# The state scan of a hybrid layer on one core: tables group by group, products for two groups at a time

## The chip, the cores and the metric

The kernel runs on one core of a Trainium2 chip. The metric is device microseconds of one execution, lower is better. A core has a matrix engine (PE in the profile; PEld is its weight load), a vector engine (DVE), a scalar engine (ACT), a general engine (POOL) and a queue that issues transfers (SP). Each works through its own list of instructions in order. The lists are made when the kernel is built: a scheduler places what the code records, and the code can pin an order.

## The reference

One layer of a streaming model for 256 frames of a new stream and 32 frames of a running one, 288 columns together:

```python
xn   = rmsnorm(x, norm_mix_pre)
proj = xn @ w_in                    # [u_pool 1024 | z 2048 | xBC 2560 | dt 32]
y_pool = pool_mixer(u_pool)         # trailing means, then a small matmul
xBC  = silu(causal_dwconv(xBC))     # xs 2048, B 256, C 256
y    = ssd_scan(xs, dt, A, B, C, h0) + D * xs      # 32 heads of 64
y    = y * silu(z);  y = y * rsqrt(mean(y*y)) * g   # mean per half of the heads
x    = x + rmsnorm([y_pool, y] @ w_out)
up   = rmsnorm(x) @ w_up;  f = (silu(conv(gate)) * conv(value)) @ w_down
x    = x + rmsnorm(f)
```

All is float32. The big products are made from two reduced parts of each operand: `hi` (rounded) and `lo` (the rest), as hi·hi + hi·lo + lo·hi.

## The kernel before

Columns of the activations are the free dimension (288), features are the partitions. A large product is a *projection* of 256 output features: 16 blocks of 128 inputs, three matmuls each, for two accumulators (`acc`, a ring of five PSUM banks). Its weights come in two transfers `raw` of 1 MB on the SP queue (ring of four), and each is split in two pieces: ACT rounds `whi` (L129), DVE subtracts for `wlo` (L130). Both are rings of four, so the split runs at most four pieces ahead of PE. One piece feeds 24 matmuls (L135, L136, L137). When a projection ends, DVE takes its two accumulators out (`ebuf` at L341/L342 for xs, `z` at L517).

The scan is done in eight groups of four heads by `ssd_four(q)`. A group fetches the decay exponents `gb`, the state `h0t` and the time-major inputs `xw` (written shortly before as `blocks`, DVE transposes at L171, through DRAM tensor `xs_d`). ACT makes the table `m`: twelve Relu (L471) and one Exp (L474). DVE scales `xw` (L466), `ce` (L463) and `m` (L476). PE then makes 16 small products into two banks `py` (L483 to L489, of the three-bank ring `aux`), in plain float32, with 64-column weights. The profile has two records for each of these float32 matmuls. DVE adds `py` to `xs` (L492).

The eight groups run between the projections. The code calls projections 1 to 7 (xs) and then 8 to 15 (z); `XS_RATE` and `Z_RATE` say after which of them a group is recorded:

```python
XS_RATE = (0, 0, 0, 1, 0, 1, 0, 1)
Z_RATE = (1, 0, 1, 0, 1, 1, 1, 0)
```

Nothing pins the products; the scheduler puts them where it finds their inputs ready. `gb`, `xw`, `h0t`, `ce` and `m` are rings of two.

Ahead of the scan stand nine transposes `ptok` of 32-row tiles (L420 to L422), which turn exponents `g`, steps `dt` and decays `dec` to time-major `tok` and `tokd`, and six float32 products `pcb` (L437 to L439) for the table `cbt`. After a group, the gate multiplies `xs` by silu(z) (L523, L526) and sums squares into `gsum`; when eight tiles are done, `gate_rstd(0)` makes a product `psum_g` (L496), a root on ACT, a reciprocal on DVE (L237), and eight multiplies (L578).

Of the kernel before, what the change touches and what calls it, by code (L numbers as in the profile page):

```python
# [8 lines left out]
F32 = mybir.dt.float32  # L9
F32R = mybir.dt.float32r  # L10
AF = mybir.ActivationFunctionType
ALU = mybir.AluOpType
# [4 lines left out]
P = 128  # L17
TC = {"schedule_with_timeline_sim": True}
D_MODEL = 2048
NP_ = 256  # L20
NS = 32
NT = NP_ + NS
# [3 lines left out]
HEADS = 32  # L26
# [3 lines left out]
NX = D_SSD // P  # L30
# [5 lines left out]
HALF = NF // 2  # L36
MW = 416
EVAC = 100
XS_RATE = (0, 0, 0, 1, 0, 1, 0, 1)
Z_RATE = (1, 0, 1, 0, 1, 1, 1, 0)  # L40


@with_exitstack
def body(
# [25 lines left out]
    act, dve, pool, pe, sp = nc.scalar, nc.vector, nc.gpsimd, nc.tensor, nc.sync  # L70
# [7 lines left out]
    acc_ps = ctx.enter_context(tc.tile_pool(name="acc_ps", bufs=5, space=PSUM))  # L78
# [3 lines left out]
    def aux(shape, name):  # L82
        return aux_ps.tile(shape, F32, tag="aux", name=name)
# [81 lines left out]
            after = nxt  # L165
        return accs

    def blocks_out(d, t, src, pool_):

        s = pool_.tile([P, NT], F32, tag="blocks", bufs=1, name="blocks")  # L170
        dve.transpose(s, src)  # L171
# [9 lines left out]
    mean = const.tile([P, P], F32, name="mean")  # L181
# [16 lines left out]
    for i in range(NE):  # L198
        e = const.tile([P, 326], F32, name=f"ebuf{i}")
# [12 lines left out]
    rstd = const.tile([P, NT], F32, tag="spread", bufs=3, name="rstd")  # L212
# [4 lines left out]
    start = ExitStack()  # L217
# [35 lines left out]
    for kb, n in chunks:  # L253
# [19 lines left out]
        for k in range(kb, kb + n):  # L273
# [19 lines left out]
            for m in range(6):  # L293
                c = slice(m * P, (m + 1) * P)
# [5 lines left out]
    p_ = aux([P, NT], "pdt")  # L300
# [18 lines left out]
    mp = mixer.enter_context(tc.tile_pool(name="mixer", bufs=1))  # L319
# [9 lines left out]
    cw = pah[:, 0:80].rearrange("p (r t) -> p r t", t=NXC)  # L329
    cb_ = pah[:, 80:100]  # L330
    n_conv = [0]
    more = [mp.tile([P, 326], F32, name=f"ebuf{NE + i}") for i in range(2)]
    for e in more:
        pool.memset(e, 0.0)

    def conv_in(i, p_):

        e = (ebuf + more)[n_conv[0] % (NE + 2)]
        n_conv[0] += 1
        with tc.high_priority(offset=EVAC):  # L340
            dve.tensor_tensor(e[:, 3:259], p_[:, :NP_], rstd[:, :NP_], op=ALU.mult)  # L341
            dve.tensor_tensor(e[:, 262:294], p_[:, NP_:], rstd[:, NP_:], op=ALU.mult)  # L342
        pool.tensor_copy(e[:, 259:262], hist_c[:, :, i])
        return e

# [72 lines left out]
    for b, (go, o) in enumerate(((0, 0), (256, P), (288, NT - P))):  # L418
        p_ = aux([P, 3, HEADS], "ptok")
        pe.transpose(p_[:, 0, :], g[:, go : go + P], id32)  # L420
        pe.transpose(p_[:, 1, :], dt[:, o : o + P], id32)
        pe.transpose(p_[:, 2, :], dec_s if b == 2 else dec[:, o : o + P], id32)  # L422
        dve.tensor_copy(tok[:, b, :, :], p_[:, 0:2, :])
        dve.tensor_copy(tokd[:, b, :], p_[:, 2, :])

    bc = []
    for i in range(4):
# [4 lines left out]
    cbt = mp.tile([P, 2, MW], F32, name="cbt")  # L432
    pool.memset(cbt, 0.0)
    for gi in range(2):
        blocks_out(b_d, gi, bc[gi], mp)
# [10 lines left out]
    xs = []  # L446
    elast = const.tile([P, HEADS + 32], F32, name="elast")

    def ssd_four(q):

        c = slice(2 * P * q, 2 * P * q + 2 * P)
        gb = mp.tile([P, 4, MW], F32, tag="gb", bufs=2, name="gb")
        sp.dma_start(out=gb, in_=g_d[4 * q : 4 * q + 4, :].unsqueeze(0).broadcast_to([P, 4, MW]))
        h0t = mp.tile([P, 2 * P], F32, tag="h0t", bufs=2, name="h0t")
        sp.dma_start(out=h0t, in_=state_ssd[:, c])
        xw = mp.tile([P, 3, 2 * P], F32, tag="xw", bufs=2, name="xw")
        sp.dma_start(out=xw[:, 0:2, :], in_=xs_d[:NP_, c].rearrange("(b p) c -> p b c", p=P))
        sp.dma_start(out=xw[:, 2, :], in_=xs_d[NT - P :, c])
        ce = mp.tile([P, 4, NS], F32, tag="ce", bufs=2, name="ce")
        act.activation(ce, gb[:, :, 384:], AF.Exp)  # L460
        act.activation(elast[:, 4 * q : 4 * q + 4], gb[:, :, MW - 1], AF.Exp)
        cs = bc[2 + q // 4][:, NP_:]
        dve.tensor_tensor(ce, ce, cs.unsqueeze(1).broadcast_to([P, 4, NS]), op=ALU.mult)  # L463
        w = tok[:, :, 1, 4 * q : 4 * q + 4].unsqueeze(3).broadcast_to([P, 3, 4, 64])
        x4 = xw.rearrange("p b (r q) -> p b r q", r=4)
        dve.tensor_tensor(x4, x4, w, op=ALU.mult)  # L466
        m = mp.tile([P, 4, MW], F32, tag="m", bufs=2, name="m")
        for j in range(4):
            h = 4 * q + j
            for b, (lo_, hi_) in enumerate(((0, 256), (256, 384), (384, MW))):  # L470
                act.activation(  # L471
                    m[:, j, lo_:hi_], gb[:, j, lo_:hi_], AF.Relu, bias=tok[:, b, 0, h : h + 1], scale=-1.0
                )
        act.activation(m, m, AF.Exp, scale=-1.0)  # L474
        gi = q // 4
        dve.tensor_tensor(m, m, cbt[:, gi : gi + 1, :].broadcast_to([P, 4, MW]), op=ALU.mult)  # L476
        ys = [aux([P, NT], "py") for _ in range(2)]
        for k in range(4):
            for j in range(4):
                c = slice(64 * j, 64 * j + 64)  # L480
                y = ys[j // 2][64 * (j % 2) : 64 * (j % 2) + 64, :]
                if k == 0:
                    pe.matmul(y[:, 0:256], xw[:, 0, c], m[:, j, 0:256], start=True, stop=False)  # L483
                elif k == 1:
                    pe.matmul(y[:, 128:256], xw[:, 1, c], m[:, j, 256:384], start=False, stop=True)  # L485
                elif k == 2:
                    pe.matmul(y[:, 256:], xw[:, 2, c], m[:, j, 384:], start=True, stop=False)  # L487
                else:
                    pe.matmul(y[:, 256:], h0t[:, c], ce[:, j, :], start=False, stop=True)  # L489
        for i in range(2):  # L490
            t = 2 * q + i
            dve.scalar_tensor_tensor(xs[t], xs[t], dcol[:, t : t + 1], ys[i], op0=ALU.mult, op1=ALU.add)  # L492

    def gate_rstd(t):
        p_ = aux([P, NT], "psum_g")
        pe.matmul(p_, mean, gsum[t], start=True, stop=True)  # L496
        o = const.tile([P, NT], F32, tag="spread", bufs=3, name="rg")
        root(o, p_, 0.5)
        return o
# [13 lines left out]
    def gate_in(t, p_):  # L513

        z = mp.tile([P, NT], F32, tag="z", bufs=4, name="z")
        with tc.high_priority(offset=EVAC):
            dve.tensor_tensor(z, p_, rstd, op=ALU.mult)  # L517
        zs[t] = z

    def gate_silu(t):  # L520
# [12 lines left out]
    def xs_conv(i):  # L533
        for j in range(2):
            o = btile("xs")
            conv_out(2 * i + j, xs_in[2 * i + j], o)
            blocks_out(xs_d, 2 * i + j, o, mp)
            xs.append(o)

    xs_d = dram.tile([NT, D_SSD], F32, name="xs_d")  # L540
# [1 line left out]
    fours = list(range(NX // 2))  # L542
    gates = list(range(NX))
    done = [-1]
    rg = []

    def run_fours(n):
        for _ in range(n):
            if fours and 2 * fours[0] + 1 < len(xs):
                q = fours.pop(0)  # L550
                ssd_four(q)
                done[0] = 2 * q + 1

    def run_gates():
        while gates and gates[0] in zs and gates[0] <= done[0]:
# [2 lines left out]
    for i in range(1, NX // 2):  # L558
        ps = project(win, [(O_X + 256 * i, 256)], xn, K16)
        xs_evac(i, ps)  # L560
        xs_conv(i - 1)
        run_fours(XS_RATE[i])
    for i in range(NX // 2):
        ps = project(win, [(O_Z + 256 * i, 256)], xn, K16)
        for j in range(2):
            gate_in(2 * i + j, ps[j])
        if i == 0:
            xs_conv(NX // 2 - 1)
        run_fours(Z_RATE[i])
        for j in range(2):  # L570
            gate_silu(2 * i + j)
        run_gates()
        if i == 4:
            assert gates[0] >= 8
            rg.append(gate_rstd(0))
        if i > 4:
            for t in range(3 * i - 15, min(8, 3 * i - 12)):
                dve.tensor_tensor(xs[t], xs[t], rg[0], op=ALU.mult)  # L578
    run_fours(NX)
    run_gates()  # L580
    assert not gates and not fours

# [666 lines left out]
```

## Time and profile before

| | |
|---|---|
| median of 3 runs | 1319.08 us (1318.94 to 1319.94) |
| profiled execution | 1318.3 us, of which the span of the trace 1316.4 us |
| PE busy | 1310.2 us |
| DVE busy | 895.7 us |
| ACT busy | 671.6 us |
| the stage that the change touches | about 90 to 290 us of the span |

A row of the timeline gives start and length in us, engine, line, operation, output<-inputs and shape; equal neighbours are merged with their count. A matmul's length reaches past the start of the next one, since they are pipelined: what a matmul costs is read from start to start. A row of groups ends with `busy us, mean ns | idle before`, and who ended that idle time.

### The profile page before, as it was taken

Reading aid. Unit: us, or ns where it says so; the run is one execution under the profiler, and the core shown is the slowest. Engines: PE = TensorE matmul, PEld = TensorE weight load, DVE = VectorE, ACT = ScalarE, POOL = GpSimd, SP = SyncE. Lnnn points to the kernel's source line nnn. Section 1 sums busy time; section 2 is a strip of 40 time slices with the busy share of each in tenths; the row PEclk is TensorE's granted clock in tenths of the full one; section 3 lists DMA queues with packets and bytes.
Section 4 is the critical chain, followed back from the end, with each engine's and each line's share of the span. In section 5 each row is a group of like instructions: output and inputs, shape, how many; then the busy total and the mean of one; then the engine's idle time right before and its main releaser. Section 6 shows DMA issues by size and latency. Waiting matters only on the chain.

```text
span 1316.4 us, 25204 instructions
## 1 busy us (share of the span) xinstructions
PE 1310.2 (100%) x10067; PEld 1298.4 (99%) x10067; DVE 895.7 (68%) x1486; ACT 671.6 (51%) x1010; POOL 229.7 (17%) x363
## 2 busy tenths in 40 slices
PE   9999999999999999999999999999999999999998
PEld 9999999999999999999999999999999999999997
DVE  8889988679654599977766744336666666664544
ACT  7558866446543466554444433334444454444443
POOL 6321221211430200211211200001111111101110
PEclk9999999999999999999999999999999999999999
DMA  9668874465665556666444445445445554466663
GB/s 350 186 209 279 278 223 145 165 221 204 208 219 181 183 167 213 187 184 203 168 161 165 160 168 173 158 171 185 168 161 165 180 169 161 163 235 187 203 179 109
DMA packets 104996, 249.81 MB, mean 190 GB/s; under 512 B 64272, under 2 KB 70352, under 8 KB 82608
## 3 DMA queue, kind: packets, MB, share of 16 engines
q1 hardware_dynamic: 102784, 243.44, 56.3%
q0 software_dynamic: 1664, 4.59, 1.2%
q8 instruction: 78, 1.28, 0.4%
q14 instruction: 38, 0.31, 0.1%
q10 hardware_dynamic: 432, 0.19, 0.1%
HBM read 236.23 MB, written 11.95 MB: 189 GB/s over the span
## 4 chain that ended last, share of the span: by engine, by line
PE 100%; ACT 0%; issue 0%; POOL 0%; DVE 0%; POOLq 0%
PE acc L135 31%; PE acc L137 31%; PE acc L136 31%; PE acc_x L137 1%; PE acc_x L135 1%; PE acc_x L136 1%; PE py L483 1%; PE pst L780 0%; PE run_a L1121 0%; PE low L1119 0%; PE idle L249 0%; PE run_b L1134 0%; PE py L485 0%; PE pdt L304 0%; PE py L489 0%; PE py L487 0%
## 5 line engine op out<-in xcount | busy, mean ns | idle before, releaser
L130 DVE TENSOR_TENSOR wlo<-raw,whi 128x1024 fp32r<-128x1024 f32 (+1 forms) x386 | 463.4, 1202 | 321.1 <-ACT whi L129 318.5
L129 ACT ACTIVATE whi<-raw 128x1024 fp32r<-128x1024 f32 (+1 forms) x386 | 400.1, 1037 | 476.8 <-PE acc L136 375.1
L135 PE MATMUL acc<-hn,whi 128*128 128x288 f32 x1360 | 393.3, 294 | 0.0
L136 PE MATMUL acc<-hn,whi 128*128 128x288 f32 x1360 | 392.7, 293 | 0.0
L137 PE MATMUL acc<-hn,wlo 128*128 128x288 f32 x1360 | 391.9, 293 | 0.0
L135 PEld LDWEIGHTS acc<-hn,whi 128*128 128x128 f32 x1360 | 253.3, 188 | 0.4 <-ACT hn L880 0.4
L136 PEld LDWEIGHTS acc<-hn,whi 128*128 128x128 f32 x1360 | 253.4, 188 | 0.1
L137 PEld LDWEIGHTS acc<-hn,wlo 128*128 128x128 f32 x1360 | 253.3, 188 | 0.0
L135 PE MATMUL acc<-xn,whi 128*128 128x288 f32 x688 | 203.2, 296 | 0.0
L136 PE MATMUL acc<-xn,whi 128*128 128x288 f32 x688 | 201.0, 293 | 0.0
L137 PE MATMUL acc<-xn,wlo 128*128 128x288 f32 x688 | 199.6, 295 | 0.0
L135 PE MATMUL acc<-fa,whi 128*128 128x288 f32 x660 | 194.0, 294 | 0.0
L136 PE MATMUL acc<-fa,whi 128*128 128x288 f32 x660 | 193.4, 293 | 0.0
L137 PE MATMUL acc<-fa,wlo 128*128 128x288 f32 x660 | 193.1, 293 | 0.0
L135 PEld LDWEIGHTS acc<-xn,whi 128*128 128x128 f32 x688 | 129.4, 188 | 1.3 <-issue 0.9
L136 PEld LDWEIGHTS acc<-xn,whi 128*128 128x128 f32 x688 | 129.2, 188 | 0.4
L137 PEld LDWEIGHTS acc<-xn,wlo 128*128 128x128 f32 x688 | 128.1, 188 | 0.0
L135 PEld LDWEIGHTS acc<-fa,whi 128*128 128x128 f32 x660 | 124.1, 188 | 0.0
L136 PEld LDWEIGHTS acc<-fa,whi 128*128 128x128 f32 x660 | 123.9, 188 | 0.0
L137 PEld LDWEIGHTS acc<-fa,wlo 128*128 128x128 f32 x660 | 123.9, 188 | 0.0
L932 POOL COPY fc_stage<-ebuf 128x4 f32<-128x4 f32 x88 | 28.4, 323 | 523.3 <-DVE ebuf L931 523.3
L928 POOL COPY ebuf<-pf 128x2 f32<-128x2 f32 x88 | 72.4, 824 | 122.2 <-DVE fc L938 70.2
(307 smaller groups left out, 1741.9 us busy)
## 6 DMA issues: line engine op xcount, KB each, us to landing
raw<-in_w_up SPq DMA_DIRECT2D x80, 1024.0 KB, 4.8
raw<-in_w_in SPq DMA_DIRECT2D x38, 1024.0 KB, 5.2
raw<-in_w_down SPq DMA_DIRECT2D x32, 1024.0 KB, 4.8
raw<-in_w_out SPq DMA_DIRECT2D x23, 1024.0 KB, 4.8
raw<-in_w_down SPq DMA_DIRECT2D x16, 768.0 KB, 4.2
raw<-in_w_up SPq DMA_DIRECT2D x8, 896.0 KB, 4.6
gb<-g_d SPq DMA_DIRECT2D x8, 832.0 KB, 6.6
raw<-in_w_first SPq DMA_DIRECT2D x5, 768.0 KB, 7.3
```

Of the source, the lines that this page charges most:

```text
L129: act.activation(hi, raw[:, k : k + n, :], AF.Copy)
L130: dve.tensor_tensor(lo, raw[:, k : k + n, :], hi.bitcast(F32), op=ALU.subtract)
L135: pe.matmul(out, wh, a[:, 0, :], start=start, stop=False)
L136: pe.matmul(out, wh, a[:, 1, :], start=False, stop=False)
L137: pe.matmul(out, wl, a[:, 0, :], start=False, stop=stop)
L483: pe.matmul(y[:, 0:256], xw[:, 0, c], m[:, j, 0:256], start=True, stop=False)
L928: pool.tensor_copy(e[:, 258:260], pf[:, 4:6, i])
L932: pool.tensor_copy(fc_stage[:, :, :, i], e[:, 256:324].rearrange("p (s c) -> p s c", c=34)[:, :, 0:2])
```

## The change

- `ssd_four` becomes `four_in(q)` (transfers, tables, scaling) and `four_out(q, ...)` (products and the add to `xs`). `SCAN_IN` names the projections after which one group's inputs are made, one group each; `SCAN_OUT` those after which the products of the two waiting groups are made, one behind the other. All 32 products are pinned in the order of the code, the first behind the waiting groups' last table multiply. The fourth bank of a pair, `py_a`, is taken from the ring `acc`.
- On DVE, `four_in`'s instructions are queued behind the last take-out of the projection just done. This is an order, not a wait.
- The nine transposes go to one bank and are pinned in one row, the decays first; two copies take the place of six.
- `blocks` has three buffers in the mixer in place of one.
- `gate_rstd(0)` is recorded behind the last pair of groups (14 instead of 12), pinned, and the eight multiplies go four at a time behind projections 14 and 15.

```diff
-XS_RATE = (0, 0, 0, 1, 0, 1, 0, 1)
-Z_RATE = (1, 0, 1, 0, 1, 1, 1, 0)
+SCAN_IN = {5, 6, 7, 8, 9, 11, 12, 13}
+SCAN_OUT = {7, 9, 12, 14}
-        s = pool_.tile([P, NT], F32, tag="blocks", bufs=1, name="blocks")
+        s = pool_.tile([P, NT], F32, tag="blocks", bufs=bufs, name="blocks")
...
+    def tok_out():
+        p_ = aux([P, 3, 3, HEADS], "ptok")
+        jobs = [(2, 2, dec_s)] + [(b, 2, dec[:, P * b : P * b + P]) for b in range(2)]
+        for b, (go, o) in enumerate(((0, 0), (256, P), (288, NT - P))):
+            jobs += [(b, 0, g[:, go : go + P]), (b, 1, dt[:, o : o + P])]
+        for n, (b, i, src) in enumerate(jobs):
+            ins = pe.transpose(p_[:, b, i, :], src, id32)
+            if n:
+                tc.keep_in_program_order(ins)
+        dve.tensor_copy(tok, p_[:, :, 0:2, :])
+        dve.tensor_copy(tokd, p_[:, :, 2, :])
...
-    def ssd_four(q):
+    def four_in(q):
...
+        with tc.issue_after(last_in[0].ins):
+            act.activation(ce, gb[:, :, 384:], AF.Exp)
...
+    def four_out(q, ys, xw, h0t, ce, m, _, after=None):
...
+        for y, w_, v_, go, end in ops:
+            with ExitStack() as order:
+                if after is not None:
+                    order.enter_context(tc.issue_after(after.ins))
+                ins = pe.matmul(y, w_, v_, start=go, stop=end)
+            tc.keep_in_program_order(ins)
+            after = None
...
+    def scan(i):
+        if i in SCAN_OUT:
+            ys = [aux([P, NT], "py") for _ in range(3)] + [acc_ps.tile([P, NT], F32, tag="acc", name="py_a")]
+            for n, (q, got) in enumerate(ready):
+                four_out(q, ys[2 * n : 2 * n + 2], *got, after=None if n else ready[-1][1][-1])
+            done[0] = 2 * ready[-1][0] + 1
+            ready.clear()
+        if i == 14:
+            assert gates[0] >= 8
+            rg.append(gate_rstd(0, True))
+        if i in SCAN_IN:
+            q = fours.pop(0)
+            assert 2 * q + 1 < len(xs)
+            ready.append((q, four_in(q)))
...
-            for t in range(3 * i - 15, min(8, 3 * i - 12)):
-                dve.tensor_tensor(xs[t], xs[t], rg[0], op=ALU.mult)
+            for t in range(4 * i - 24, 4 * i - 20):
+                with tc.issue_after(last_in[0].ins):
+                    dve.tensor_tensor(xs[t], xs[t], rg[0], op=ALU.mult)
```

What this does to the engines' lists, at three places. First PE's products for a group. In the list of before, the fourth group (`py` are its two banks):

```order
L137 MATMUL acc<-xn,wlo 128x288
L483 MATMUL py<-m,xw 64x256 x4
L485 MATMUL py<-m,xw 64x128 x4
L487 MATMUL py<-m,xw 64x32 x4
L489 MATMUL py<-ce,h0t 64x32 x4
L135 MATMUL acc<-xn,whi 128x288
```

In the changed kernel's PE list, the first pair of groups, behind projection 7:

```order
L137 MATMUL acc<-xn,wlo 128x288
L506 MATMUL py<-m,xw 64x256 x4
L506 MATMUL py<-m,xw 64x128 x4
L506 MATMUL py<-m,xw 64x32 x4
L506 MATMUL py<-ce,h0t 64x32 x4
L506 MATMUL py<-m,xw 64x256 x2
L506 MATMUL py_a<-m,xw 64x256 x2
L506 MATMUL py<-m,xw 64x128 x2
L506 MATMUL py_a<-m,xw 64x128 x2
L506 MATMUL py<-m,xw 64x32 x2
L506 MATMUL py_a<-m,xw 64x32 x2
L506 MATMUL py<-ce,h0t 64x32 x2
```

Two more heads' `ce` products into `py_a` follow, then `acc` again. PE's list had groups in nine places (one was cut into two halves with projection matmuls between) and has them in four, of two groups each.

Second, the transposes on PE. In the list of before the first six of them stand so, and the other three in two more places further on:

```order
L137 MATMUL acc<-xn,wlo 128x288
L420 MATMUL ptok<-ident,g 128x32
L421 MATMUL ptok<-ident,dt 128x32
L135 MATMUL acc<-xn,whi 128x288
L420 MATMUL ptok<-ident,g 128x32
L421 MATMUL ptok<-ident,dt 128x32
L420 MATMUL ptok<-ident,g 128x32
L421 MATMUL ptok<-ident,dt 128x32
L136 MATMUL acc<-xn,whi 128x288
```

In the changed list the nine are one row, whose end is this, and `pcb` follows at once:

```order
L425 MATMUL ptok<-ident,g 128x32
L425 MATMUL ptok<-ident,dt 128x32
L444 MATMUL pcb<-bc 128x256
L445 MATMUL pcb<-bc 128x128
L446 MATMUL pcb<-bc 128x32
```

Transposes stood in four places and `pcb` in a fifth; now all stand in one.

Third, DVE behind a group's products. In the list of before, from the add of `py` to the second weight piece after it:

```order
L492 SCALAR_TENSOR_TENSOR xs<-xs,par_119,py 128x288 x2
L463 TENSOR_TENSOR ce<-ce,bc 128x128
L354 SCALAR_TENSOR_TENSOR conv<-ebuf_115,pah,conv 128x291
L354 SCALAR_TENSOR_TENSOR conv<-ebuf_117,pah,conv 128x291
L130 TENSOR_TENSOR wlo<-raw,whi 128x1024
L476 TENSOR_TENSOR m<-m,cbt 128x1664
```

In the changed list, the end of what stands between two weight pieces behind the first pair (ahead of it are the first three of the four adds of `py`, `ce` and two `conv`):

```order
L511 SCALAR_TENSOR_TENSOR xs<-xs,par_119,py_a 128x288
L355 SCALAR_TENSOR_TENSOR conv<-ebuf_117,pah,conv 128x291
L475 TENSOR_TENSOR xw<-xw,tok 128x768
L360 SCALAR_TENSOR_TENSOR xs<-tanh,conv 128x256
L361 SCALAR_TENSOR_TENSOR xs<-tanh,conv 128x32
L171 STREAM_TRANSPOSE blocks<-xs 128x288
L484 TENSOR_TENSOR m<-m,cbt 128x1664
L360 SCALAR_TENSOR_TENSOR xs<-tanh,conv 128x256
L361 SCALAR_TENSOR_TENSOR xs<-tanh,conv 128x32
L130 TENSOR_TENSOR wlo<-raw,whi 128x1024
```

Four adds, `xw` and `m` now stand in front of one weight piece; before, a weight piece stood between the adds and `m`.

More of the change, by code (lines that the diff above doesn't have):

```diff
@@ L331, in body @@
     n_conv = [0]
+    last_in = [None]
     more = [mp.tile([P, 326], F32, name=f"ebuf{NE + i}") for i in range(2)]
@@ L417, in body @@
     dec_s = dec_s.rearrange("h r s -> h (r s)")
[L418 to L424, printed above, removed]
+    def tok_out():
[9 more added lines that the diff above has]
+        dve.tensor_copy(tokd, p_[:, :, 2, :])
+    tok_out()
     bc = []
@@ L459, in ssd_four @@
         ce = mp.tile([P, 4, NS], F32, tag="ce", bufs=2, name="ce")
[L460 to L466, printed above, removed]
-        m = mp.tile([P, 4, MW], F32, tag="m", bufs=2, name="m")
[L468 to L477, printed above, removed]
+        m = mp.tile([P, 4, MW], F32, tag="m", bufs=2, name="m")
+        with tc.issue_after(last_in[0].ins):
+            act.activation(ce, gb[:, :, 384:], AF.Exp)
+            act.activation(elast[:, 4 * q : 4 * q + 4], gb[:, :, MW - 1], AF.Exp)
+            cs = bc[2 + q // 4][:, NP_:]
+            dve.tensor_tensor(ce, ce, cs.unsqueeze(1).broadcast_to([P, 4, NS]), op=ALU.mult)
+            w = tok[:, :, 1, 4 * q : 4 * q + 4].unsqueeze(3).broadcast_to([P, 3, 4, 64])
+            x4 = xw.rearrange("p b (r q) -> p b r q", r=4)
+            dve.tensor_tensor(x4, x4, w, op=ALU.mult)
+            for j in range(4):
+                h = 4 * q + j
+                for b, (lo_, hi_) in enumerate(((0, 256), (256, 384), (384, MW))):
+                    act.activation(
+                        m[:, j, lo_:hi_], gb[:, j, lo_:hi_], AF.Relu, bias=tok[:, b, 0, h : h + 1], scale=-1.0
+                    )
+            act.activation(m, m, AF.Exp, scale=-1.0)
+            gi = q // 4
+            got = dve.tensor_tensor(m, m, cbt[:, gi : gi + 1, :].broadcast_to([P, 4, MW]), op=ALU.mult)
+        return xw, h0t, ce, m, got
+    def four_out(q, ys, xw, h0t, ce, m, _, after=None):
+        ops = []
         for k in range(4):
@@ L492, in ssd_four, with gate_rstd @@
             dve.scalar_tensor_tensor(xs[t], xs[t], dcol[:, t : t + 1], ys[i], op0=ALU.mult, op1=ALU.add)
-    def gate_rstd(t):
+    def gate_rstd(t, pin=False):
         p_ = aux([P, NT], "psum_g")
-        pe.matmul(p_, mean, gsum[t], start=True, stop=True)
+        ins = pe.matmul(p_, mean, gsum[t], start=True, stop=True)
+        if pin:
+            tc.keep_in_program_order(ins)
         o = const.tile([P, NT], F32, tag="spread", bufs=3, name="rg")
@@ L536, in xs_conv @@
             conv_out(2 * i + j, xs_in[2 * i + j], o)
-            blocks_out(xs_d, 2 * i + j, o, mp)
+            blocks_out(xs_d, 2 * i + j, o, mp, 3)
             xs.append(o)
@@ L544, in body @@
     done = [-1]
+    ready = []
     rg = []
[L547 to L552, printed above, removed]
+    def scan(i):
[12 more added lines that the diff above has]
+            ready.append((q, four_in(q)))
     def run_gates():
@@ L561, in body @@
         xs_conv(i - 1)
-        run_fours(XS_RATE[i])
+        scan(i)
     for i in range(NX // 2):
@@ L568, in body @@
             xs_conv(NX // 2 - 1)
-        run_fours(Z_RATE[i])
+        scan(NX // 2 + i)
         for j in range(2):
```

22 lines of the change are left out of this document (9 added, 13 removed).

## The prediction

> **What bounds the kernel now.** I began with the page and with PE's waits, since one engine holds the whole span.
>
> ```profile
> span 1316.4 us, 25204 instructions
> PE 1310.2 (100%) x10067; PEld 1298.4 (99%) x10067; DVE 895.7 (68%) x1486; ACT 671.6 (51%) x1010; POOL 229.7 (17%) x363
> ```
> ```profile
> PE idle L249 <- POOL mean L182: 1.2, 1, 1.2
> PE y_ps L1164 <- ACT diag L1163: 0.6, 1, 0.6
> ```
>
> PE waits for others 1.8 us in all, at the first and the last instructions. Between them it never waits, so the kernel gets faster only where PE has less to do, and slower only where DVE, ACT or a transfer is late for it. The stretch view gives the price of a projection matmul:
>
> ```profile
> 600.00:1200.00 600.00, 600.00 (x4578) 1.00 0.51 172
> ```
>
> 600 us for 4578 of them is 0.131 us each, at a granted clock of 1.00; a weight piece (24) is 3.15 us.
>
> The change touches PE at its short float32 products, so next I read PE's timeline around them. First one whole group of four heads, then the one that the scheduler cut in two:
>
> ```profile
> 142.96 0.29 PE L137 MATMUL acc<-xn,wlo 128*128 128x288 f32 x1
> 143.18 1.08 PE L483 MATMUL py<-m,xw 128*64 128x256 f32 x8
> 144.09 0.61 PE L485 MATMUL py<-m,xw 128*64 128x128 f32 x8
> ...
> 145.07 0.40 PE L135 MATMUL acc<-xn,whi 128*128 128x288 f32 x1
> 145.31 0.29 PE L136 MATMUL acc<-xn,whi 128*128 128x288 f32 x1
> 145.44 0.29 PE L137 MATMUL acc<-xn,wlo 128*128 128x288 f32 x1
> ```
> ```profile
> 124.53 0.29 PE L135 MATMUL acc<-xn,whi 128*128 128x288 f32 x1
> 124.75 0.65 PE L483 MATMUL py<-m,xw 128*64 128x256 f32 x4
> 125.24 0.39 PE L485 MATMUL py<-m,xw 128*64 128x128 f32 x4
> ...
> 126.13 0.29 PE L135 MATMUL acc<-xn,whi 128*128 128x288 f32 x1
> ...
> 129.69 0.29 PE L135 MATMUL acc<-xn,whi 128*128 128x288 f32 x1
> ...
> 131.28 0.30 PE L135 MATMUL acc<-xn,whi 128*128 128x288 f32 x1
> ```
>
> From 142.96 to 145.44 is 2.48 us with three projection matmuls in it (0.39), so the whole group costs 2.09. The halves cost 1.60 - 0.39 = 1.21 and 1.59 - 0.39 = 1.20, together 2.41. The same 16 products cost 0.32 more when PE goes into them twice: 0.32 is the price of one entry. The rows show where it lies: the first `py` starts 0.22 behind the last `acc` and not 0.13, and on the way out 145.07 to 145.31 is 0.24.
>
> **The change part by part.** *Products of two groups in one row.* Nine entries become four: 5 x 0.32 = 1.60 us less. The upper end: in the whole group the first two heads at 256 columns take 124.75 to 125.24 = 0.49 (read in the half, same shapes), the next two 0.91 - 0.49 = 0.42. So the entry has 0.09 ahead of it, 0.07 inside and 0.11 behind the first `acc`; for the step from the last product to that `acc`, which no row parts off, I allow as much as for the step in, 0.09. That is 0.36 for each of the four joins of whole groups, 1.76 with the undone cut. The lower end, if a second group had to be entered anew, is the undone cut alone, 0.32. I take 1.70, since the halves are the nearest rows.
>
> [...]
>
> *Transposes in one row.* The rows of their four places and of `pcb`:
>
> ```profile
> 97.06 0.29 PE L137 MATMUL acc<-xn,wlo 128*128 128x288 f32 x1
> ...
> 97.85 0.24 PE L420 MATMUL ptok<-ident,g 32*128 32x32 f32 x1
> ...
> 98.06 0.22 PE L421 MATMUL ptok<-ident,dt 32*128 32x32 f32 x1
> ...
> 98.58 0.30 PE L135 MATMUL acc<-xn,whi 128*128 128x288 f32 x1
> ```
> ```profile
> 102.53 0.29 PE L135 MATMUL acc<-xn,whi 128*128 128x288 f32 x1
> ...
> 103.22 0.29 PE L137 MATMUL acc<-xn,wlo 128*128 128x288 f32 x1
> ```
> ```profile
> 104.95 0.29 PE L135 MATMUL acc<-xn,whi 128*128 128x288 f32 x1
> ...
> 105.58 0.30 PE L137 MATMUL acc<-xn,wlo 128*128 128x288 f32 x1
> ```
> ```profile
> 107.70 0.29 PE L135 MATMUL acc<-xn,whi 128*128 128x288 f32 x1
> ...
> 109.85 0.30 PE L135 MATMUL acc<-xn,whi 128*128 128x288 f32 x1
> ```
>
> Six transposes cost 1.52 - 0.52 = 1.00, two cost 0.69 - 0.26 = 0.43, one 0.63 - 0.26 = 0.37: 1.80 for nine; `pcb` costs 2.15 - 0.39 = 1.76. In a row they start 0.07 apart (97.85 to 98.06 for four), so the nine alone are 0.65 and the four entries 1.15, or 0.29 each. Now there is one entry, 0.87 less, and its way out leads into `pcb`, which has its own; that can save up to a further half entry. I take 0.95, between 0.85 and 1.05. Two copies on DVE for six cost PE nothing: DVE is off PE's path there.
>
> *The gate's sum.* Alone it is
>
> ```profile
> 269.31 0.29 PE L137 MATMUL acc<-xn,wlo 128*128 128x288 f32 x1
> 269.44 0.65 PE L496 MATMUL psum_g<-gsum,mean 128*128 128x288 f32 x2
> ...
> 270.19 0.30 PE L137 MATMUL acc<-xn,wlo 128*128 128x288 f32 x1
> ```
>
> 0.88 - 0.39 = 0.49, with no entry price (0.13 ahead of it). Before, the first `psum_g` followed a group directly; now four projection matmuls stand between. I put it at no change. But it needs the first of three `py` banks back: DVE's first add of the pair must be done 0.5 us after the pair. Let T0 be the end of projection 14 on PE. DVE's work up to that add, from the groups by form in the scan's stretch (90 to 260 us):
>
> ```profile
> L130 DVE TENSOR_TENSOR wlo<-raw,whi 128x1024 fp32r<-128x1024 f32 x48 | 59.4, 1241 | 10.4 <-ACT whi L129 10.0
> L523 DVE SCALAR_TENSOR_TENSOR z<-tanh_z,z 128x288 f32<-128x288 f32 x16 | 9.7, 616 | 0.1
> L492 DVE SCALAR_TENSOR_TENSOR xs<-xs,par,py 128x288 f32<-128x288 f32 x16 | 7.6, 508 | 0.0
> L517 DVE TENSOR_TENSOR z<-acc,rstd 128x288 f32<-128x288 f32 x16 | 7.1, 452 | 1.6 <-PE acc L137 1.6
> ```
>
> A take-out, a `z` step, a weight piece, a `z` step and the add are 0.45 + 0.62 + 1.24 + 0.62 + 0.51 = 3.4 us; `psum_g` stands at T0 + 3.8 + 0.5 = 4.3. It fits by about 1 us; if not, PE stands still that long, once.
>
> *What the new order asks of DVE and ACT.* More rows of those groups, and ACT behind a group on the timeline:
>
> ```profile
> L476 DVE TENSOR_TENSOR m<-m,cbt 128x1664 f32<-128x1664 f32 x8 | 15.4, 1925 | 0.5 <-ACT m L474 0.5
> L466 DVE TENSOR_TENSOR xw<-xw,tok 128x768 f32<-128x768 f32 x8 | 7.6, 954 | 3.6 <-DMA xw<-xs_d 3.6
> L171 DVE STREAM_TRANSPOSE blocks<-xs 128x288 f32<-128x288 f32 x14 | 6.6, 474 | 4.3 <-DMA xs_d<-blocks 4.2
> ```
> ```profile
> 144.95 1.92 ACT L471 ACTIVATE m<-gb,tok 128x256 f32<-128x256 f32 x6 [0.33 <-PE py L487]
> ...
> 148.79 1.05 ACT L129 ACTIVATE whi<-raw 128x1024 fp32r<-128x1024 f32 x1
> 149.74 1.58 ACT L474 ACTIVATE m<-m 128x1664 f32<-128x1664 f32 x1
> ```
>
> ACT waits for the products (`<-PE py`), because `m` has two buffers, and then works 144.95 to 148.79 = 3.84 us on a group's Relu. In the changed list both groups' Relu and one Exp stand ahead of the next `whi`. With T0 now the end of projection 7 on PE: Relu can start at T0 + 1.8 (144.95 against 143.18), the two groups take 7.7, the Exp 1.6, `whi` 1.05: T0 + 12.2. PE needs that piece after the pair (3.8 us) and four pieces (12.6): T0 + 16.4. On DVE, `m` follows the Exp (T0 + 11.1, then 1.9), a short `xs` step (0.5) and the piece (1.2): T0 + 14.7 against 16.4 + 0.26, as the third matmul is the first to use `wlo`. That leaves 2.0 us. Two pieces later on PE (6.3 us), DVE has done those two pieces (2.4) and in between a second `m` (1.9), an `xw` (0.95), two take-outs (0.9) and four short steps, about 5 us: 1 us of cover is left. That is the tightest place; behind the second and third pair I find about 2 us, since no `m` of a second group follows so soon. So I count this at nothing: what hides it is the four pieces that PE still has, and beyond 1 us of delay each us costs a us.
>
> Edits with one answer: three `blocks` buffers end the 4.2 us for which DVE stood at L171, worth nothing to PE, which did not wait, but it is cover. On SP, `h0t` and `xw` of the next groups wait for the pair to end, with a `raw` of weights behind them; that `raw` is needed some ten pieces (30 us) later. The reciprocal of the gate moves behind the last pair; the next weight piece behind it on DVE is for four pieces later. The order's list for the tail of the program is the same.
>
> Sum: 1.70 + 0.95 = 2.65 us. The profiled execution (1318.3, with 1316.4 of span) would be 1315.6. It lies 0.8 below the median of the runs, so against the median I forecast 1319.08 - 2.65 = **1316.4**. A difference of 0.2% (2.64 us) is about what a measurement of this kernel can tell from no change: the forecast stands right on that edge.
>
> **The rivals.** (1) *The joins save little.* If the 32-column products at a group's end force the next group's first product to be entered anew, only the undone cut and the transposes count: 0.32 + 0.95 = 1.3 us, 1317.8, within 0.2%. Against it: inside a group the step from head to head and from shape to shape costs nothing that the rows show. For it: no row has a 32-column product ahead of a 256-column one.
>
> (2) *The cover is gone: slower.* Place: the weight piece behind the two groups' tables on ACT and DVE. [...] A late `xw` or Exp holds all weight pieces that stand behind it. If the tables come 4 us later than worked out behind each of three pairs (L466 already waited 3.6 us for its transfer over eight groups, and now two such transfers are issued together), PE loses 4 - 1 = 3, 4 - 2 = 2 and 2 us: 1316.4 + 7 = 1323.4. It ends over 0.2% slower from about 3.5 us of delay. Against it: before, the same chain for one group made PE wait nowhere.
>
> (3) *A little of it.* 1 us at `psum_g`, or 2 us of delay behind the first pair: 1317.4 to 1318, within 0.2%.
>
> That the change does not do what it says is out: in the list the pairs and the transposes stand unbroken.
>
> **How the numbers follow.** Forecast case 0.62, of which, being on the edge, 0.50 faster and 0.12 within 0.2%; rival 1 0.13; rival 3 0.10; rival 2 0.15. So faster 0.50, same 0.35, slower 0.15. The range: below, the upper ends 1.76 + 1.05 = 2.8 and the scatter of the runs (0.8, by the profiled execution) give 1315.5; above, rivals 1 and 3 lie within 1318, and with stalls of up to some 4 us it reaches 1320.5. What is left out is most of rival 2 and little below.
>
> **What would show it.** In the timeline of the changed kernel a pair of groups should cost 4.18 - 0.32 = 3.8 to 3.9 us by the same count, and the second group start 0.05 to 0.1 behind the last `ce` product, where rival 1 has 0.3. The transposes with `pcb` should cost 2.6 (1.76 and 0.85). PE's list of waits should still have only the two rows; a row `PE acc <- DVE wlo` or `<- ACT whi` in the four pieces behind a pair would be rival 2, `PE psum_g <- DVE xs` rival 3. The forecast is wrong if PE's extra time outside these places changes.

## The result, and the profile after

The changed kernel takes 1316.46 us in the median (13 runs, 1315.98 to 1318.03), the kernel before, measured beside it, 1319.08 (13 runs, 1318.46 to 1320.25). The ratio is 0.9979, with a 95% interval of 0.9972 to 0.9986: 2.62 us less, where 2.65 was worked out. So the kernel is faster; whether by more than the 0.2% on which the forecast stood is open, since 0.998 lies inside the interval.

The page and PE's waits of the changed kernel:

```profile
span 1314.8 us, 25188 instructions
PE 1308.6 (100%) x10067; PEld 1298.2 (99%) x10067; DVE 891.9 (68%) x1482; ACT 671.5 (51%) x1010; POOL 222.0 (17%) x363
```
```profile
PE idle L249 <- POOL mean L182: 1.2, 1, 1.2
PE y_ps L1191 <- ACT diag L1190: 0.6, 1, 0.6
```

The list has its two old rows and no third: nothing is late behind a pair. Next PE's timeline, first around the first pair of groups, then around the transposes (start, length; equal neighbours merged):

```profile
138.31 0.29 PE L137 MATMUL acc<-xn,wlo 128*128 128x288 f32 x1
138.54 1.73 PE L506 MATMUL py<-m,xw 128*64 128x256 f32 x24
140.09 0.40 PE L506 MATMUL py<-ce,h0t 128*64 128x32 f32 x8
140.32 0.63 PE L506 MATMUL py<-m,xw 128*64 128x256 f32 x4
...
142.19 0.40 PE L135 MATMUL acc<-xn,whi 128*128 128x288 f32 x1
142.43 0.29 PE L136 MATMUL acc<-xn,whi 128*128 128x288 f32 x1
142.56 0.29 PE L137 MATMUL acc<-xn,wlo 128*128 128x288 f32 x1
```
```profile
104.56 0.29 PE L137 MATMUL acc<-xn,wlo 128*128 128x288 f32 x1
104.79 0.24 PE L425 MATMUL ptok<-ident,dec_s 32*128 32x32 f32 x1
...
105.46 0.70 PE L444 MATMUL pcb<-bc 128*128 128x256 f32 x2
...
107.59 0.30 PE L137 MATMUL acc<-xn,wlo 128*128 128x288 f32 x1
```

The pair costs 142.56 - 138.31 - 3 x 0.131 = 3.86, where two whole groups cost 2 x 2.09 = 4.18. The other three pairs cost 3.85 to 3.86 in the same count. The transposes with `pcb` cost 107.59 - 104.56 - 0.39 = 2.64, before 1.80 + 1.76 = 3.56. Summed from the trace's unrounded starts over all such places, PE's extra time fell by 1.61 us at the groups and 0.93 at the transposes, 2.54 in all.

The two spans differ by only 1.6. The reason lies at the start, which the change does not touch: the same product `prs` in the two timelines, before and after.

```profile
38.55 0.65 PE L241 MATMUL prs<-xsum,mean 128*128 128x288 f32 x2
```
```profile
39.36 0.65 PE L241 MATMUL prs<-xsum,mean 128*128 128x288 f32 x2
```

The profiled execution of the changed kernel came 0.8 us later to it, and 2.54 - 0.8 = 1.7 is nearly the difference of the spans. Its first projection matmuls stood 0.24 apart up to 6.9 us, where those of before stood 0.13 apart:

```profile
5.99 0.44 PE L135 MATMUL acc<-xn,whi 128*128 128x288 f32 x1
6.23 0.44 PE L136 MATMUL acc<-xn,whi 128*128 128x288 f32 x1
```

How an execution begins differs from run to run (`prs` starts between 38.5 and 39.7 us in the traces of this case), so the medians are the better measure of the change. Counted from `prs` to the end of the span, which leaves the start out, the kernel before takes 1316.4 - 38.55 = 1277.9 us and the changed one 1314.8 - 39.36 = 1275.4, so 2.4 less (2.43 unrounded). The 0.1 that is missing to 2.54 is spread over the projection matmuls. Further down this count is called the time from `prs` on.

### The profile page after: what moved, and what is told of

Read it like the earlier page. It is cut to its first block, busy times and chain, and to the rows that moved or that the text cites. A ratio compares the mean times of both kernels' runs of the same rounds, so it can differ in the third digit from the quotient of the medians.

```text
span 1314.8 us, 25188 instructions
## 1 busy us (share of the span) xinstructions
PE 1308.6 (100%) x10067; PEld 1298.2 (99%) x10067; DVE 891.9 (68%) x1482; ACT 671.5 (51%) x1010; POOL 222.0 (17%) x363
## 4 chain that ended last, share of the span: by engine, by line
PE 100%; ACT 0%; issue 0%; POOL 0%; DVE 0%; POOLq 0%
PE acc L135 31%; PE acc L137 31%; PE acc L136 31%; PE py L506 1%; PE acc_x L137 1%; PE acc_x L135 1%; PE acc_x L136 1%; PE pst L807 0%; PE run_a L1148 0%; PE low L1146 0%; PE idle L249 0%; PE run_b L1161 0%; PE py_a L506 0%; PE pdt L304 0%; PE low L136 0%; PE low L135 0%
## 5 line engine op out<-in xcount | busy, mean ns | idle before, releaser
L965 DVE SCALAR_TENSOR_TENSOR fc<-ebuf,pf,fc 128x290 f32<-128x290 f32 x176 | 90.1, 517 | 2.8 <-ACT fc L963 0.2
```

The costliest lines, as they stand in the source:

```text
L965: dve.scalar_tensor_tensor(c, e[:, r_ : r_ + 290], pf[:, r_, i : i + 1], c, op0=ALU.mult, op1=ALU.add)
```

## The experiments

Time differences below are between medians. Each label's text is what was on record before it ran. In expectations "cover" is the time by which a weight piece is ready ahead of its first use on PE.

**The two savings apart.** `e1_pairs` is the changed kernel with the transposes of before; `e3_single` is the changed kernel with one group's products at a time.

```diff
 e1_pairs
-    tok_out()
+    for b, (go, o) in enumerate(((0, 0), (256, P), (288, NT - P))):
+        p_ = aux([P, 3, HEADS], "ptok")
...
 e3_single
-SCAN_OUT = {7, 9, 12, 14}
+SCAN_OUT = {7, 8, 9, 10, 11, 12, 13, 14}
...
+            q, got = ready.pop(0)
+            four_out(q, [aux([P, NT], "py") for _ in range(2)], *got, after=got[-1])
```

> The changed kernel with the transposes as they were, in four places, with six copies. Entry theory: the four pairs stay at 3.86 us each as in the changed kernel's trace (15.42 in all, against 17.04 before), and the transposes with pcb go back from 2.63 to about 3.56 us: 1316.46 + 0.93 = 1317.4 us. Rival (the row of transposes gives PE nothing, the gain is all from the pairs): no change from the changed kernel, 1316.5.

> The changed kernel with the products of one group at a time, pinned as before, behind projections 7 to 14; all else is as in the changed kernel. Entry theory: eight entries for four, each group at 2.09 us (16.7 for 15.42 in all), so 1316.46 + 1.3 = 1317.8 us, with PE waiting nowhere. Rival (the gain is from the new order of the tables or the third blocks buffer): as the changed kernel, 1316.5.

Measured: `e1_pairs` 1317.50 us (1316.88 to 1318.74; ratio to before 0.9986, 0.9977 to 0.9995), so the row is worth 1.04. `e3_single` 1317.46 (1316.97 to 1319.07; 0.9989, 0.9980 to 0.9998), so four joins are worth 1.0. PE's timeline of `e3_single` at its first group:

```profile
137.82 0.29 PE L137 MATMUL acc<-xn,wlo 128*128 128x288 f32 x1
138.04 1.73 PE L506 MATMUL py<-m,xw 128*64 128x256 f32 x24
139.59 0.41 PE L506 MATMUL py<-ce,h0t 128*64 128x32 f32 x8
...
140.30 0.29 PE L137 MATMUL acc<-xn,wlo 128*128 128x288 f32 x1
```

140.30 - 137.82 - 0.39 = 2.09 again, for each of the eight groups. Four joins save 8 x 2.09 - 4 x 3.86 = 1.3 of PE's time. The medians alone leave room, since the intervals of these two kernels and of the changed one overlap. The profiled executions say the same: from `prs` on both take 1276.5 us, where the changed kernel takes 1275.4 and the kernel before 1277.9. So both terms of the sum reach the time.

**The row alone.** The kernel before, with the nine transposes in one row and nothing else.

```diff
-    for b, (go, o) in enumerate(((0, 0), (256, P), (288, NT - P))):
...
+    def tok_out():
...
+    tok_out()
```

> The kernel before with only the transposes in one row. In its list the scheduler no longer cuts a group in two, so the groups have eight entries and not nine. Entry theory: transposes with pcb 2.63 us for 3.56, and one entry of 0.32 less: 1319.08 - 0.93 - 0.32 = 1317.8 us. Rival (the row gives nothing): 1319.1, or 1318.8 for the undone cut alone.

Measured: 1322.51 us (1320.42 to 1325.06), ratio 1.0024 (1.0015 to 1.0033). It is slower than before, against both expectations. The row itself costs what it should in the trace (`ptok` and `pcb` 2.62), and the cut group is whole in this list, but PE now waits, and so does DVE. PE's waits, then DVE's between 90 and 260 us, then DVE's timeline:

```profile
PE acc L137 <- DVE wlo L130: 2.3, 2, 1.6
```
```profile
DVE blocks L171 <- DMA xs_d<-blocks: 9.6, 6, 3.4
```
```profile
183.20 0.48 DVE L171 STREAM_TRANSPOSE blocks<-xs 128x288 f32<-128x288 f32 x1 [3.45 <-DMA xs_d<-blocks]
```

The list was made anew around the row, and in it the `blocks` transposes meet their one buffer still in flight: 9.6 us of waiting, 4.2 before. After the 3.45 us at 183 us DVE has no idle time left that its timeline shows until PE stands for `wlo`, 1.6 us at 201 us and 0.7 at 205.

**How many buffers.** The changed kernel with one and with two `blocks` buffers.

```diff
-        blocks_out(b_d, gi, bc[gi], mp, 3)
+        blocks_out(b_d, gi, bc[gi], mp)        # e5_blocks1; ", mp, 2)" in e10_b2
-            blocks_out(xs_d, 2 * i + j, o, mp, 3)
+            blocks_out(xs_d, 2 * i + j, o, mp)
```

> The changed kernel with one blocks buffer, as before. The prediction's view (it is cover only): DVE again stands a few us at the transposes into blocks, PE waits nowhere, 1316.5 us as the changed kernel. Rival (with pairs this cover is needed): PE's matmuls behind a pair or near 120 us are spread out by up to 2.5 us, 1317 to 1319.

> The changed kernel with two blocks buffers in place of three (with one it came out at 1318.94 us, PE waiting 2.1 us in three places near 120 to 126 us). If what counts is that the transfer out of a buffer, some 4 us, must not stand between two block transposes in a row (they come in pairs), two buffers do: 1316.5 us, PE waiting nowhere behind a pair. Rival: three in a row are in flight at once and the third still stops DVE: 1317 to 1318.5, with a wlo or whi row in PE's list of waits.

Measured: one buffer 1318.94 us (1316.71 to 1321.38; ratio 0.9999, 0.9991 to 1.0008), two buffers 1316.30 (1315.81 to 1317.12; 0.9980, 0.9971 to 0.9988). With one buffer the whole gain is gone: the prediction's view of the buffers, 1316.5, failed, and the rival came true. PE's waits and DVE's with one buffer:

```profile
PE acc L137 <- DVE wlo L130: 1.4, 2, 0.9
...
PE acc L135 <- ACT whi L129: 0.7, 1, 0.7
```
```profile
DVE blocks L171 <- DMA xs_d<-blocks: 7.9, 7, 2.8
```

PE's three waits end at 120.44, 124.80 and 126.47 us, all ahead of the first pair (141 us), where the first groups' tables stand between the weight pieces. The second buffer is worth 2.6 us, the third nothing that can be told.

**Buffers in the kernel before.** Three buffers alone (`e9_b3`), and with the row (`e8_row_b3`).

```diff
-        blocks_out(b_d, gi, bc[gi], mp)
+        blocks_out(b_d, gi, bc[gi], mp, 3)
-            blocks_out(xs_d, 2 * i + j, o, mp)
+            blocks_out(xs_d, 2 * i + j, o, mp, 3)
```

> The kernel before with three blocks buffers in the scan and nothing else (transposes in four places, one group of products at a time, the cut group still cut). My prediction's view, the buffers are worth nothing to PE as long as PE does not wait: 1319.05 within 0.3 us, with the DVE wait at the block transposes (4.2 us) gone. Rival: runs of before other than the profiled one do lose time to that wait, so that the median falls by 0.5 us or more, to 1318.5 or less, and the scatter of the runs (1318.0 to 1320.9) narrows.

> The kernel before with the nine transposes in one row and, this time, three blocks buffers in the scan. The row alone, with one buffer, came out at 1322.5 us, slower than before, and in its trace DVE stands 9.6 us at the block transposes, once 3.4 us at 183 us, and PE then stands 1.6 and 0.7 us for wlo at 201 and 205 us. Buffer theory: that wait is the cause; with three buffers DVE does not stand there, PE's list of waits is down to its first and last row, and what is left is the row's own 0.93 us: 1319.05 - 0.93 = 1318.1 us (the cut group is still cut in this list). Rival, the order theory: the list that comes out of the new row is a bad one whatever the buffers; PE still waits for wlo near 200 us and the time stays at 1320.5 to 1322.5.

Measured: `e9_b3` 1320.34 us (1318.94 to 1324.75), ratio 1.0018 (1.0008 to 1.0028); `e8_row_b3` 1319.45 (1317.81 to 1324.15), 1.0003 (0.9995 to 1.0012). Buffers that remove a wait made the kernel before slower. With the row they are 3.1 us faster than the row with one buffer, PE's waits for `wlo` are gone from the profiled execution, and the row's own saving shows against `e9_b3` (0.9 us); but the loss that the buffers bring (1.3 us) is larger. Neither kernel met an expectation. The runs spread over 6 us. In `e9_b3` the profile shows where the wait went, DVE's waits first, then its timeline, then PE's:

```profile
DVE xw L466 <- DMA xw<-xs_d: 10.4, 5, 4.5
```
```profile
133.29 0.96 DVE L466 TENSOR_TENSOR xw<-xw,tok 128x768 f32<-128x768 f32 x1 [4.49 <-DMA xw<-xs_d]
...
139.45 1.22 DVE L130 TENSOR_TENSOR wlo<-raw,whi 128x1024 fp32r<-128x1024 f32 x1
```
```profile
140.86 0.30 PE L137 MATMUL acc<-xn,wlo 128*128 128x288 f32 x1
```

L171 waits no longer, but `xw` waits 10.4 us where it waited 3.6: it reads through DRAM what `blocks` has just written. In the old order the multiply comes soon after, and weight pieces stand behind it. One is ready at 139.45 + 1.22 = 140.67, and PE uses it at 140.86, 0.2 us later; the same reading gives 0.2 or 0.3 at two more pieces, where before the least was 2.3. This profiled execution just passed: from `prs` on it takes 1277.95 us, the kernel before 1277.87. With a transfer a little later PE would stand, which would give the times up to 1324.75; no trace of such an execution was taken, so this is argued and not shown.

**The waiting multiply out of DVE's list.** Both kernels again, with `xw` scaled on POOL.

```diff
-        dve.tensor_tensor(x4, x4, w, op=ALU.mult)
+        pool.tensor_tensor(x4, x4, w, op=ALU.mult)
```

> The kernel before with three blocks buffers, and the multiply of xw moved from DVE to POOL. With three buffers alone it came out at 1320.34 us (runs up to 1324.75), and in its trace DVE's wait had moved from the block transposes (4.2 us before, now none) to the multiply of xw (3.6 us before, now 10.4), with weight pieces queued behind it that come only 0.2 us ahead of PE. Queue theory: it is that the weight pieces stand behind the waiting multiply; taken out of DVE's list, the weight pieces are early again, and the time is that of before, 1319.05, or a little less, with runs within 1318 to 1320.5. Rival: something else in this order, such as the transfers themselves or ACT's pieces, is late in the slow runs: 1320.3 with runs up to 1324 as without the move. In a third case POOL, behind its own waits, is late with xw: PE waits at py.

> The same move on the kernel before with the transposes in one row and three blocks buffers, which came out at 1319.45 us (runs up to 1324.15) where 1318.1 was expected. Queue theory: 1319.05 - 0.93 = 1318.1 us, with runs within 1317.3 to 1319.5, so that the saving that PE's list has always shown reaches the time. Rival: 1319.4 and runs up to 1324 as without the move.

Measured: `e11_b3_pool` 1319.28 us (1318.36 to 1319.79), ratio 1.0000 (0.9991 to 1.0009); `e12_row_b3_pool` 1317.89 (1317.39 to 1320.04), 0.9994 (0.9985 to 1.0003). The highest time is 5.0 us lower in the first and 4.1 in the second, and the row's saving is there: 1.4 us between the two medians, 1.0 between the profiled executions from `prs` on (ahead of it PE waits 0.4 and 1.0 us for ACT's first pieces, a part that the move does not touch). In the first, POOL now does the waiting for the transfer, and DVE's longest wait is for ACT's rounded pieces (POOL's waits, then DVE's, then the piece with the least cover on DVE and on PE):

```profile
POOL xw L466 <- DMA xw<-xs_d: 25.9, 4, 17.8
```
```profile
DVE wlo L130 <- ACT whi L129: 12.7, 9, 2.3
```
```profile
145.97 1.21 DVE L130 TENSOR_TENSOR wlo<-raw,whi 128x1024 fp32r<-128x1024 f32 x1
```
```profile
148.98 0.30 PE L137 MATMUL acc<-xn,wlo 128*128 128x288 f32 x1
```

That piece is ready at 147.18, 1.8 us ahead, where `e9_b3` had 0.2 at its tightest. With the row the same reading does not part the two: the least is 0.4 in `e8_row_b3` and 0.5 in `e12_row_b3_pool`, and yet the runs of the second spread far less. In the first the tight piece stands behind a wait of 3.60 us for the transfer, in the second behind none, which fits, but one profiled execution of each is too little to show it.

By the medians, a transfer waited for on POOL cost nothing that the time shows, and the same one on DVE 1.1 and 1.6 us. This fits a list worked through in order: in `e9_b3` DVE did nothing in its wait of 4.49 us for `xw`, and its next weight piece, at 135.03, came behind the multiply. One reservation: the move also takes 8 x 0.95 = 7.6 us of work from DVE and makes the list anew, so wait and work are not parted. It is not free either: where POOL's multiply ran beside them, DVE's passes took longer, `m` 3.08 us at 142.53 in `e11_b3_pool` for 1.93, and the tight piece of `e12_row_b3_pool` 2.10 for 1.21.

**The cover spent on purpose.** One (`e4_m1`) or two (`e4_m2`) more DVE passes over each group's table `m`, each of 1.9 us, before its multiply (the maximum of `m` with itself, which leaves the values alone).

```diff
+            for _ in range(1):          # range(2) in e4_m2
+                dve.tensor_tensor(m, m, m, op=ALU.max)
```

> The changed kernel with one DVE instruction more in each group's inputs: a maximum of m with itself, as long as the table multiply (1.97 us) and just ahead of it. The places with the least cover in the changed kernel's trace are the third weight piece behind the first pair (1.49 us, two tables ahead of it), the first piece behind the second pair (2.06) and behind the third (2.67), and the pieces near 120 us (2.8). Cover theory: PE stands 2 x 1.97 - 1.49 = 2.4 us behind the first pair, and nowhere else: 1316.46 + 2.4 = 1318.9 us. Rival (the pieces are not what PE waits for, or DVE's idle time takes it up): 1316.5.

> The same with two such maxima, 3.93 us more for each group. Cover theory: behind the first pair 2 x 3.93 - 1.49 = 6.4 us, behind the second 3.93 - 2.06 = 1.9, behind the third 1.3, near 120 us about 1.1: 1316.46 + 10.7 = 1327 us, slower than the kernel before, at the places that the prediction's second rival names. Rival (delays add up otherwise, or PE takes them up): under 1321.

Measured: 1320.51 us (1318.51 to 1321.50; ratio 1.0006, 0.9997 to 1.0016) and 1330.65 (1329.57 to 1332.93; 1.0090, 1.0073 to 1.0107). Against the runs of before on the same chip (1319.42) they are 1.1 and 11.2 us slower, so that against the changed kernel, 2.6 us faster than before, 3.7 and 13.9 us are lost, where 2.4 and 10.7 were expected (the second kernel has only four runs). The order of size is as expected. The place is not. PE's waits of the one and of the other:

```profile
PE py L508 <- DVE m L486: 2.2, 1, 2.2
```
```profile
PE py L508 <- DVE m L486: 7.9, 2, 4.3
```

No piece behind a pair was late. PE stood inside the third pair in the first kernel, and inside the first and third in the second, for the second group's own `m`: the new list put weight pieces ahead of the longer tables and let the tables be late. The piece that the expectation named, the third behind the first pair, came near it in the first kernel:

```profile
160.67 2.35 DVE L130 TENSOR_TENSOR wlo<-raw,whi 128x1024 fp32r<-128x1024 f32 x2
```
```profile
162.10 0.29 PE L137 MATMUL acc<-xn,wlo 128*128 128x288 f32 x1
```

The first of the two pieces is ready at 161.89, so 0.2 us of cover is left of 1.5. The dose ate that cover without making PE wait for it in this execution, so what a delay beyond the cover costs there was not tested. Of the 3.7 us, the profiled execution shows 2.4 at the third pair; the rest lies in runs without a trace and stays open.

**What an entry costs, measured by itself.** The changed kernel with each of the gate's two means made in two 64-column halves in place of one 128-column product.

```diff
-        ins = pe.matmul(p_, mean, gsum[t], start=True, stop=True)
+        for c in (slice(0, 64), slice(64, P)):
+            ins = pe.matmul(p_[c, :], mean[:, c], gsum[t], start=True, stop=True)
```

> The changed kernel with the product of the gate's sum, twice in the program, made in two halves of 64 columns and not at once with 128. The streaming is the same, since the two column tiles work side by side. Tiling theory (the entry price belongs to the change to 64-column tiles): each psum_g costs its 0.49 us and an entry of about 0.3 more, 0.8 us. Rival (the price belongs to short products or to float32): 0.49 to 0.55 us.

Measured, in one execution: 1316.39 us; it also began 0.8 us earlier than the profiled execution of the changed kernel, so the price is read at the place:

```profile
241.74 0.29 PE L135 MATMUL acc<-xn,whi 128*128 128x288 f32 x1
241.96 0.71 PE L516 MATMUL psum_g<-gsum,mean 128*64 128x288 f32 x4
...
242.97 0.30 PE L135 MATMUL acc<-xn,whi 128*128 128x288 f32 x1
```

242.97 - 241.74 - 0.39 = 0.84, against 0.49 in one product: 0.35 more, and 0.22 ahead of it where it was 0.13. The two halves run beside each other (their records start 7 ns apart, in two pairs), and what is left is the entry, 0.35 us here. The weight loads (PEld) around the changed kernel's first pair show a part of what that price is:

```profile
138.18 0.19 PEld L137 LDWEIGHTS acc<-xn,wlo 128*128 128x128 f32 x1
138.53 0.41 PEld L506 LDWEIGHTS py<-m,xw 128*64 128x64 f32 x6 [0.16 <-issue]
```
```profile
142.19 0.19 PEld L135 LDWEIGHTS acc<-xn,whi 128*128 128x128 f32 x1
```

Among projection matmuls a load begins 0.13 us ahead of its matmul (138.18 for 138.31). On the way into the pair it begins with the product (138.53 and 138.54), and on the way out with the matmul (142.19 both): at these two changes of tiles no weights are loaded ahead. From `prs` on `e6_halves` takes 0.7 us more than the changed kernel, for its two products.

## Why the prediction was right

- **Products of two groups in one row.** Right in kind, 0.09 too large: 1.61 for 1.70. The halves had given 5 x 0.32 = 1.60, and the reason that the prediction gives for 1.70, that the halves are the nearest rows, speaks for that figure. What it added, the allowance of up to 0.04 more at each join for the step out of the products, was not there. A pair cost 3.85 to 3.86 where 3.8 to 3.9 was said. The second group's first product starts at 140.32; the last two `ce` start 0.06 ahead of it, as they do from one another. Rival 1 (a second entry, 0.3) is out.
- **Transposes in a row.** 0.93 for 0.95; 2.63 with `pcb` where 2.6 was said. `e1_pairs` puts it at 1.04 in the time.
- **The gate's sum.** No change, as said: 0.49 at both places, and no wait for the bank in PE's list.
- **The chain on DVE and ACT.** Counted at nothing, and it was nothing. The estimate by hand was close. The piece named tightest, the third behind the first pair, in DVE's timeline and PE's:

```profile
159.04 1.22 DVE L130 TENSOR_TENSOR wlo<-raw,whi 128x1024 fp32r<-128x1024 f32 x1
```
```profile
161.75 0.30 PE L137 MATMUL acc<-xn,wlo 128*128 128x288 f32 x1
```

  It was ready at 160.26, 1.5 us ahead, where 1 was worked out. At the first piece it was 2.3 (2.0 was worked out), behind the second and third pair 2.1 and 2.7 (about 2).
- **Three buffers.** "Worth nothing to PE, but it is cover" was half right, and the half with a price was missing. Cover that is not needed before can be needed after: without a second buffer the new list loses 2.6 us (`e5_blocks1`). Rival 2 named the right mechanism, a transfer that holds DVE with weight pieces behind it, but at another transfer and another place: with one buffer it comes true, at `blocks` (7.9 us of DVE's waits, and 2.1 of PE's) and ahead of the first pair, not behind one. DVE's groups by form of the changed kernel, 90 to 260 us, show where DVE waits now:

```profile
L484 DVE TENSOR_TENSOR m<-m,cbt 128x1664 f32<-128x1664 f32 x8 | 15.7, 1965 | 7.0 <-ACT m L482 7.0
L475 DVE TENSOR_TENSOR xw<-xw,tok 128x768 f32<-128x768 f32 x8 | 7.6, 954 | 5.2 <-DMA xw<-xs_d 5.2
L171 DVE STREAM_TRANSPOSE blocks<-xs 128x288 f32<-128x288 f32 x14 | 6.3, 464 | 0.0
```

  The transfers out of `blocks` and into `xw` together hold DVE 5.2 us (the 7.0 at `m` is for ACT, with no weight piece late behind it); before it was 4.2 + 3.6 = 7.8, in `e9_b3` 10.4. So in these runs the buffers and the new place of the multiply belong together: buffers without it made the kernel before slower, the whole change without them gained nothing.
- **The base.** Setting the sum against the median, and not against the profiled execution, was the right choice, since the two profiled executions differ by 0.8 us at their start alone. That the medians differ by 2.62 where the sum was 2.65 is luck in part: the interval is 1.8 us wide, the sum was 0.1 too large at the entries, and the profiled executions give 2.43 from `prs` on.

No version that was run beats the changed kernel by what can be told; with two buffers it is as fast (1316.30 and 1316.46).

## What to carry to other kernels

Where one engine never waits, its list can be summed from start to start in the timeline, and grouping short products of one shape saved a price for each entry, here 0.3 us; but the saving reaches the time only while the engines that feed it keep their cover, so read that cover piece by piece, from the end of the feeder to the first use. A wait that is taken away can come back at the next transfer that the engine waits for, as it did here on DVE (4.2 us less at `blocks`, 6.8 more at `xw`), and what stands behind it in the list is the place to look for its cost: with the waiting multiply out of DVE's list the time was 1.1 and 1.6 us less. A spread of the runs that grows from 2 us to 6, as in `e9_b3` and `e8_row_b3`, can be a sign that the cover is used up, even when the profiled execution shows no wait: the least cover there was 0.2 and 0.4 us, though that it made the spread was argued and not shown.

## What the runs showed of the hardware

PE's granted clock fell at some of its waits and not at others. Stretches of `e4_m2` inside and behind a wait of 3.55 us (140.70 to 144.25) and behind one of 4.34 (up to 222.43), and of `e4_m1` behind one of 2.22 (busy time and count of PE, PEld, DVE, ACT, POOL, then the clock, DMA share and rate):

```profile
140.70:143.40 2.70, 0.00 (x1) 0.00 (x0) 2.70 (x3) 2.70 (x10) 2.70 (x1) 1.00 0.86 314
143.50:150.30 6.80, 6.05 (x42) 5.24 (x43) 6.80 (x16) 6.05 (x15) 1.62 (x4) 0.50 0.95 332
144.30:150.40 6.10, 6.10 (x43) 5.28 (x44) 6.10 (x16) 5.35 (x13) 0.82 (x3) 0.51 0.96 353
150.40:156.50 6.10, 6.10 (x48) 6.10 (x48) 6.10 (x9) 5.62 (x12) 0.00 (x0) 1.00 0.57 129
222.10:225.40 3.30, 2.97 (x24) 2.21 (x26) 3.22 (x7) 2.33 (x6) 3.14 (x3) 0.50 0.69 276
225.50:230.00 4.50, 4.50 (x44) 4.46 (x41) 4.50 (x7) 4.50 (x15) 0.43 (x1) 1.00 0.39 120
```
```profile
213.80:220.00 6.20, 6.14 (x64) 5.81 (x65) 6.20 (x14) 6.18 (x20) 2.13 (x2) 1.00 1.01 347
```

After 3.55 us without work the clock was 0.51 for the next 6.1 us, so the wait cost nearly twice as long as it lasted: the first pair of `e4_m2` took 9.55 us for 3.86, 5.69 more, and the projection matmuls behind it about 0.9 more. Behind the longer wait the clock was back at 225.4, 3.0 us after PE began again; that pair took 9.83 us, 5.97 more. So in these two the slow pace lasted no longer behind the longer wait: 3.0 us of PE's work for 6.1. Waits of 2.22 us, and of 1.59 in `e2_row`, left the pace as it was (the clock at 1.00 behind the first, the projection matmuls 0.13 apart again from 201.43 on behind the second); those of 3.55 and 4.34 did not. The clock did not fall where the wait began: in that of 3.55 us it was at 1.00 up to 143.4 and 0.50 from 143.5 on, 2.8 us after PE had stopped. Behind that wait the projection matmuls stood 0.24 apart (148.22 to 150.13). The same spacing is seen in PE's rows at the start of an execution, for some 1.1 us in the changed kernel's (from 5.75 us) and in none of the rows of before, but there the granted clock reads 1.00, so a common cause is not shown; by these rows it makes some 0.5 of the 0.8 us by which these two differ there.
